# A block of three mixers in float32: long convolution in two parts, side work moved to the attention, softmax scale on a diagonal matrix

## The chip, the cores and the metric

The kernel runs on one core of one Trainium2 chip. The metric is the device time of one execution in microseconds (us); the median of several runs is compared. A profile is one execution of its own. The engines are named as in the profile: PE is TensorE's matmul, PEld its weight load, DVE is VectorE, ACT is ScalarE, POOL is GpSimd, SP the engine that issues nearly all loads.

## What is computed

One layer of a diffusion backbone for 256 latent tokens of width 2048, with 256 context tokens beside them. The normalised and modulated tokens go through one input projection, whose columns serve three mixers: neighbourhood attention (8 heads of 128, the local window and all context keys in one softmax), a two-dimensional Fourier transform, and a gated long convolution (Hyena, 512 channels, two convolutions one after the other). Each result is normalised, an output projection follows, and then a gated MLP. What the change touches, cut from the reference:

```python
q, k, v, f, hy = split_projection(h @ w_in[l])

def long_conv(z, k_spec, bias):
    y = jnp.fft.irfft(jnp.fft.rfft(zf, n=2 * L, axis=1) * k_spec, n=2 * L, axis=1)[:, :L]
    return (y + zf * bias).astype(z.dtype)

def hyena_mix(u, conv_w, conv_b, k_spec, bias):
    u = dwconv_centred(u, conv_w, conv_b)
    v, x1, x2 = jnp.split(u, HY_ORDER + 1, axis=-1)
    z = x1 * long_conv(v, k_spec[:, 0], bias[0])
    return x2 * long_conv(z, k_spec[:, 1], bias[1])

# in the attention, for each head
p = jax.nn.softmax(s, axis=-1)
out = p_local @ v_window + p_context @ v_context

# the modulation, of which the later parts are the kernel's side work
mod = silu(c) @ ada_w + ada_b
```

## The kernel before, in words

**Products with split weights.** The large products are done in three matmuls of a faster float32 form (mm3, line 164): weights and activations are each split into a high and a low part, and high x high, high x low and low x high are summed. A weight chunk is 4 x 128 rows by 512 columns. It arrives in two halves of 512 KB (Weights.loads, line 271) into eight raw buffers; ACT makes the high part w_hi (line 173) and DVE the low part w_lo (line 174) of each half; there are two split chunks (w1, line 307). Stream.get (line 294) sees to it that the next chunk's split is issued too. One chunk is 48 matmuls of 256 columns.

**Side work.** Three of the modulation's vectors are not needed at the start: G1, A2 and B2. ada_cols (line 342) computes them in 96 small steps, each a load of 512 KB (line 350) and one DVE instruction that multiplies it with the row s_row and sums it up (line 351). The steps wait in a list, and pump(n) (line 360) issues the next 2n of them. CFG says where: `p1` in the first stage, `win` as a fraction of a pump for each of the 24 chunks of the input projection (Stream.ready, line 298), `att` as pumps after each head, `wa` in the output projection's second half, and `rest` before the MLP. The side loads share the raw buffers and SP's queue with the weights.

**The projection and the long convolution** (lines 654 to 809). After keys and values come the Fourier columns, and then the steps named in `hyo`, in this order: u0, u1 and u2 are projections of four chunks each followed by the short convolution (project, line 789; conv, line 692), q0 and q1 the queries (line 796), l0 and l1 the two long convolutions, g0 and g1 the gates (line 786), n the group norm, m the bias's mask. longconv (line 752) turns z with transposes into zt, does the forward transform in fold (line 176: four float32 products of 512 columns, sums on DVE into X), multiplies with the filter's spectrum on DVE (lines 767 to 774, tiles X and Y), and does the inverse with 16 float32 products of 128 columns (line 780, tables gtab), which DVE adds to z (line 784).

**The attention** (lines 846 to 870). For each of 8 heads and each half t of the queries: one float32 product of 512 columns (line 850), bias and scale on DVE and ACT (lines 852, 853), the maximum on DVE (line 855), Exp with its sum on ACT (line 856), the reciprocal on DVE (line 857), the scaling of the 128 x 512 scores on DVE (line 858), four transposes of 128 x 128 on TensorE against the unit matrix `ident` (line 861), and a copy to PT on ACT (line 862). Then four products with the values (line 865). Between the heads, `pace` places chunks of the output projection's first half (wout_chunk, line 833), which reads the Fourier and Hyena results, yB.

**Order.** The program gives instructions in the order of the code; a list scheduler then fixes the order on each engine ahead of the run: of what its model of time holds for ready, it takes what stands earlier in the code. On the chip each engine runs its list in order.

Of the kernel before, what the change touches and what calls it, by code (L numbers as in the profile page):

```python
# [8 lines left out]
F32 = mybir.dt.float32  # L9
F32R = mybir.dt.float32r  # L10
AF = mybir.ActivationFunctionType
ALU = mybir.AluOpType
# [23 lines left out]
for _n, _k in V_LAYOUT:  # L36
# [9 lines left out]
    ns=2,  # L46
    p1=(0, 0, 2, 6, 9),
    blocks=(2, 2, 4, 4, 4),
    win=0.8,
    att=(1, 0, 1, 4, 0, 1, 0, 0),  # L50
    rest=99,
    start='hp pk x0 x1 h3 dc ft a00 a01 a10 a11 W wm si n1s wp n2s q0 ct c0 c1 f0 e s0 n0 e f1 e s1 e h0 w q1 n1 h1',
    warm=(8, 2),
# [1 line left out]
    g2=0.34,  # L55
    pace=(0, 2, 2, 2, 3, 4, 5, 5, 6),
    wo=1,
    hyo='b u0 l0 u1 g0 u2 l1 q0 g1 n q1 m',
    ia=1,
    ib=1,  # L60
    n0=-2.0,
# [64 lines left out]
def hybrid_block(ctx: ExitStack, tc: tile.TileContext, a: dict, out: bass.AP):  # L126
# [42 lines left out]
    def transpose(ps, src, n=P):  # L169
        nc.tensor.transpose(ps, src, ident[:n, :n])  # L170
# [576 lines left out]
    with ExitStack() as st:  # L747
        hp = pool(st, "hyena", 1, "right")
        u = [hp.tile([P, 4, L], F32, name=f"u{j}") for j in range(3)]
        z = u[0]  # L750

        def longconv(o):
            zt = hp.tile([P, 2, HYW], F32, tag="zt", name="zt")
            for t in range(2):
                ps = bank()
                for c in range(4):
                    transpose(ps[:, c * P : (c + 1) * P], z[:, c, t::2])
                nc.scalar.copy(zt[:, t, :], ps[:])
            X = hp.tile([P, 4, HYW], F32, tag="X", name="X")
            Y = hp.tile([P, 4, HYW], F32, tag="Y", name="Y")  # L760
            fold(zt, Y[:, 0:2, :], X)
            k = spec[:, o]
            def both(z):
                return z.unsqueeze(1).to_broadcast([P, 2, HYW])

            for h in range(2):
                TT(Y[:, h::2, :], both(X[:, h, :]), k[:, h::2, :], op=ALU.mult)  # L767
                TT(X[:, h, :], X[:, 2 + h, :], k[:, 2 + h, :], op=ALU.mult)
                TT(X[:, 2 + h, :], X[:, 2 + h, :], k[:, h, :], op=ALU.mult)
            TT(Y[:, 0:2, :], Y[:, 0:2, :], X[:, 0:2, :], op=ALU.subtract)  # L770
            TT(Y[:, 2:4, :], Y[:, 2:4, :], X[:, 2:4, :], op=ALU.add)
            for i, op in enumerate((ALU.add, ALU.subtract, ALU.subtract, ALU.add)):
                j = 2 * (i % 2)
                TT(X[:, i, :], Y[:, j, :], Y[:, j + 1, :], op=op)  # L774
            for c in range(0, 4, 2):
                ps = bank()
                for i in range(2):
                    for t in range(2):
                        for f in range(2):
                            mm(ps[:, i * L + t * P : i * L + (t + 1) * P], X[:, 2 * t + f, (c + i) * P : (c + i + 1) * P], gtab[:, 2 * t + f, :], f == 0, f == 1)  # L780
                for i in range(2):
                    b = vec[:, V_HYB + o * 4 + c + i : V_HYB + o * 4 + c + i + 1]
                    zc = z[:, c + i, :].rearrange("p (n t) -> p t n", t=2)
                    STT(zc, zc, b, ps[:, i * L : (i + 1) * L].rearrange("p (t n) -> p t n", t=2), op0=ALU.mult, op1=ALU.add)

        def gated(gate):
            TT(z[:], z[:], gate[:], op=ALU.mult)

        def project(j):
            pss = wide(stream, 4 + 4 * j, hx_hi, hx_lo)  # L790
            for i in range(4):
                n = 4 * j + i
                wv = [vec[:, V_HCW + 12 * q + n : V_HCW + 12 * q + n + 1] for q in range(3)]
                conv(pss[i // 2][:, (i % 2) * L : (i % 2 + 1) * L], u[j][:, i, :], *wv, vec[:, V_HCB + n : V_HCB + n + 1])

        def queries(j):
            pss = wide(stream, 16 + 4 * j, hx_hi, hx_lo)
            for h in range(2):
                nc.scalar.copy(flip(qT[:, 4 * j + 2 * h : 4 * j + 2 * h + 2, :].rearrange("p i n -> p (i n)")), pss[h].rearrange("p (r c) -> p r c", c=GW))

        steps = {
            "b": make_bias,
            "u0": lambda: project(0), "u1": lambda: project(1), "u2": lambda: project(2), "q0": lambda: queries(0), "q1": lambda: queries(1),
            "l0": lambda: longconv(0), "l1": lambda: longconv(1), "g0": lambda: gated(u[1]), "g1": lambda: gated(u[2]),
            "n": lambda: group_norm(hp, [z[:, i, :] for i in range(4)], V_MIX + 12, yB, None, 4, squares4(hp, z[:], "zt")),
            "m": mask_bias,
        }
        for step in CFG["hyo"].split():
            steps[step]()
# [10 lines left out]
    with ExitStack() as st:  # L820
        ap_ = pool(st, "att", 1, "right")
        yA_hi, yA_lo = (ap_.tile([P, 8, L], F32R, name=f"yA_{z}") for z in ("hi", "lo"))
        aT = ap_.tile([P, NH, L], F32, name="aT")
        yB_hi = ap_.tile([P, 8, L], F32R, name="yB_hi")
        yB_lo = ap_.tile([P, 8, L], F32R, name="yB_lo")
        for i in range(0, 8, 2):
            split(yB_hi[:, i : i + 2, :], yB_lo[:, i : i + 2, :], yB[:, i : i + 2, :])
        sqa = ap_.tile([P, L], F32, name="sqA")
        pad(ap_, PADS["att"])
        held = {}  # L830
        x_parts = []

        def wout_chunk(h, n, kc):
            yh, yl = ((yB_hi, yB_lo), (yA_hi, yA_lo))[h]
            if kc == 0:
                held[n] = [bank(acc_ps) for _ in range(2)]
            wide_chunk(stream, h * 8 + n * 2 + kc, held[n], yh, yl, kc * 4, kc == 0, kc == 1, h * kc == 1 and n == 3)
            if kc == 1:
                add_scaled(held[n], n, G1)
            if h == 1:  # L840
                pump(CFG["wa"][2 * n + kc])
            if h == 1 and kc == 1:
                square_parts(ap_, n, x_parts, "PT", 2)

        scale = 128.0 ** -0.5
        for hd in range(NH):
            PT = ap_.tile([P, 4, L], F32, tag="PT", name="PT", bufs=2)
            for t in range(2):
                ps = bank(acc_ps)
                mm(ps[:], qT[:, hd, t * P : (t + 1) * P], kT[:, hd, :], True, True)  # L850
                s = ap_.tile([P, 512], F32, tag="s", name="s", bufs=3)
                STT(s[:, :L], ps[:, :L], scale, bias[:, hd, 2 - 2 * t : 6 - 2 * t, :].rearrange("p m c -> p (m c)"), op0=ALU.mult, op1=ALU.add)
                nc.scalar.activation(s[:, L:], ps[:, L:], AF.Copy, scale=scale)
                sm = ap_.tile([P, 3], F32, tag="sm", name="sm", bufs=3)
                nc.vector.tensor_reduce(sm[:, 0:1], s[:], axis=AX.X, op=ALU.max, negate=True)
                nc.scalar.activation(s[:], s[:], AF.Exp, bias=sm[:, 0:1], accum_out=sm[:, 1:2])
                nc.vector.reciprocal(sm[:, 2:3], sm[:, 1:2])
                TS(s[:], s[:], sm[:, 2:3], None, op0=ALU.mult)
                ps = bank()
                for j in range(4):  # L860
                    transpose(ps[:, j * P : (j + 1) * P], s[:, j * P : (j + 1) * P])
                nc.scalar.copy(PT[:, :, t * P : (t + 1) * P], ps.rearrange("p (j n) -> p j n", n=P))
            ps = bank()
            for j in range(4):
                mm(ps[:, :L], v_t[:, j, hd * P : (hd + 1) * P], PT[:, j, :], j == 0, j == 3)
            nc.scalar.copy(flip(aT[:, hd, :]), ps[:, :L].rearrange("p (r c) -> p r c", c=GW))
            square_into(ap_, sqa, aT[:, hd, :], hd == 0)
            for c in range(CFG["pace"][hd], CFG["pace"][hd + 1]):
                wout_chunk(0, c // 2, c % 2)
            pump(CFG["att"][hd])  # L870
        group_norm(ap_, [aT[:, i, :] for i in range(NH)], V_MIX, yA_hi, yA_lo, 0, [sqa])
        for c in range(CFG["pace"][NH], 8):
            wout_chunk(0, c // 2, c % 2)
        for n in range(4):
            for kc in range(2):
                wout_chunk(1, n, kc)
        pump(CFG["rest"])
        rb2 = rms_bcast(ap_, x_parts, D, "r2", fill=(8, 5))
        STT(A2[:], A2[:], 1.0, vec[:, V_N2 : V_N2 + KT], op0=ALU.add, op1=ALU.mult)
        h2_hi = rtile("C", [P, KT, L], F32R, "h2_hi")  # L880
        h2_lo = rtile("D", [P, KT, L], F32R, "h2_lo")
        for k in range(KT):
            t = modulate(ap_, xr[:, k, :], A2[:, k : k + 1], rb2[:])
            shift_split(t, B2[:, k : k + 1], h2_hi[:, k, :], h2_lo[:, k, :])
# [178 lines left out]
```

## Time and profile before

| | us |
|---|---|
| median of three runs | 1299.75 (1296.78 to 1327.46) |
| the profiled execution's own time | 1298.77 |
| its span, first to last instruction | 1297.0 |
| TensorE busy in the span | 1271.9 (98%) |
| DVE busy | 887.0 (68%) |
| ACT busy | 557.6 (43%) |
| mean HBM traffic | 242 GB/s |

The keys and values take until about 281 us, the Fourier part and the projection with the long convolutions until about 431 us, the attention until about 505 us, the rest of the output projection until about 562 us, and the MLP to the end.

How to read the rows. In a list of groups stand line, engine, operation, output and inputs, size, count, then busy us and the mean ns of one, then the engine's idle time ahead of them and what ended it. In a table by stage stand the stretch and its length, then the busy us of PE, PEld, DVE, ACT and POOL with counts, the granted clock, the share of the DMA engines and GB/s. In an order of time stand the start, the duration, and the instruction, with the number of equal ones that were merged. In the chain that ended last stand start, duration and what was on it. In a list of waits stand who waited for whom, the total us, how many times, and the longest. A matmul's duration contains the way through the array, so that the durations of neighbours overlap; how many follow one another in a time is read from their starts.

### The profile page before, as it was taken

To read this page: it belongs to the slowest core of one execution; us is meant where nothing else is said; L and a number is where in the kernel's file an instruction comes from. 1 tells how busy PE (TensorE), PEld (TensorE's weight loads), DVE (VectorE), ACT (ScalarE), POOL (GpSimd) and SP (SyncE) were. 2 spreads that over 40 slices of the span, in tenths; PEclk is the share of its full clock that TensorE was granted. 3 is DMA by queue.
4 is the path that set the end of the run, shared out by engine and by line. 5 is a ranking of instruction groups with operands and counts; after the bars stand their busy time and mean duration, and the time that the engine had idled before them with its cause. 6 is when DMAs were issued, how large, how long until landed. Compare 5 with 4: busy or idle time off the path is not lost.

```text
span 1297.0 us, 24499 instructions
## 1 busy us (share of the span) xinstructions
PE 1271.9 (98%) x10290; PEld 1195.4 (92%) x10290; DVE 887.0 (68%) x1301; ACT 557.6 (43%) x736; POOL 0.9 (0%) x7
## 2 busy tenths in 40 slices
PE   9899999999989999999999999999999999999997
PEld 5677788899889889999999999999999999999997
DVE  5446678958999898987676767744446555655563
ACT  3532213134433665455444444433334444454443
POOL 0000000000000000000000000000000000000000
PEclk9999999999999999999999999999999999999999
DMA  9888787997678875756877777855556656665541
GB/s 349 340 323 290 297 339 291 338 281 286 219 256 309 326 240 181 259 173 220 273 251 267 252 263 254 297 194 194 192 194 193 192 193 193 194 194 195 194 163 65
DMA packets 94015, 315.28 MB, mean 243 GB/s; under 512 B 16080, under 2 KB 16336, under 8 KB 93264
## 3 DMA queue, kind: packets, MB, share of 16 engines
q1 hardware_dynamic: 93328, 312.65, 69.6%
q8 instruction: 80, 1.31, 0.4%
q10 hardware_dynamic: 576, 1.07, 0.2%
q14 instruction: 31, 0.25, 0.1%
HBM read 311.58 MB, written 2.10 MB: 242 GB/s over the span
## 4 chain that ended last, share of the span: by engine, by line
PE 88%; DVE 6%; DMA 2%; SPq 1%; ACT 1%; issue 1%; DVEq 0%; ACTq 0%
PE acc_ps L162 82%; PE mi_ps L162 3%; PE mi_ps L495 2%; DVE w_lo L174 1%; SPq L648 1%; PE mi_ps L170 1%; DMA raw<-in_ada_col_t 1%; DVE raw L351 1%; DMA raw<-in_w_in_t 1%; SPq L268 0%; ACT w_hi L173 0%; DMA pack<-in_pack 0%; ACT kT L461 0%; DVE Y L767 0%; DVE X L774 0%
## 5 line engine op out<-in xcount | busy, mean ns | idle before, releaser
L173 ACT CAST w_hi<-raw 128x1024 fp32r<-128x1024 f32 x376 | 380.6, 1049 | 517.8 <-PE acc_ps L162 464.8
L174 DVE TENSOR_TENSOR w_lo<-raw,w_hi 128x1024 fp32r<-128x1024 f32 x376 | 447.8, 1220 | 214.4 <-ACT w_hi L173 211.7
L162 PE MATMUL acc_ps<-h_hi,w_hi 128*128 128x256 f32 x1408 | 388.5, 276 | 0.5 <-ACT h_hi L256 0.5
L162 PE MATMUL acc_ps<-h_lo,w_hi 128*128 128x256 f32 x1408 | 388.8, 276 | 0.0
L162 PE MATMUL acc_ps<-h_hi,w_lo 128*128 128x256 f32 x1408 | 388.7, 276 | 0.0
L162 PEld LDWEIGHTS acc_ps<-h_hi,w_hi 128*128 128x128 f32 x1408 | 264.1, 188 | 0.7 <-ACT h_hi L256 0.7
L162 PEld LDWEIGHTS acc_ps<-h_lo,w_hi 128*128 128x128 f32 x1408 | 264.3, 188 | 0.0
L162 PEld LDWEIGHTS acc_ps<-h_hi,w_lo 128*128 128x128 f32 x1408 | 264.3, 188 | 0.0
L162 PE MATMUL acc_ps<-yh,w_lo 128*128 128x256 f32 x704 | 194.4, 276 | 0.0
L162 PE MATMUL acc_ps<-yl,w_hi 128*128 128x256 f32 x704 | 194.4, 276 | 0.0
L162 PE MATMUL acc_ps<-yh,w_hi 128*128 128x256 f32 x704 | 194.4, 276 | 0.0
L351 DVE SCALAR_TENSOR_TENSOR raw<-raw,s_row 128x1024 f32<-128x1024 f32 x128 | 154.2, 1217 | 35.7 <-DMA raw<-in_ada_col_t 35.5
L162 PE MATMUL acc_ps<-hx_hi,w_hi 128*128 128x256 f32 x512 | 142.9, 281 | 2.4 <-ACT hx_hi L256 2.4
L162 PE MATMUL acc_ps<-hx_hi,w_lo 128*128 128x256 f32 x512 | 141.9, 280 | 2.6 <-DVE w_lo L174 2.6
L162 PE MATMUL acc_ps<-hx_lo,w_hi 128*128 128x256 f32 x512 | 142.6, 280 | 0.0
L162 PEld LDWEIGHTS acc_ps<-yh,w_lo 128*128 128x128 f32 x704 | 132.2, 188 | 0.0
L162 PEld LDWEIGHTS acc_ps<-yh,w_hi 128*128 128x128 f32 x704 | 132.2, 188 | 0.0
L162 PEld LDWEIGHTS acc_ps<-yl,w_hi 128*128 128x128 f32 x704 | 132.2, 188 | 0.0
L162 PEld LDWEIGHTS acc_ps<-hx_hi,w_hi 128*128 128x128 f32 x512 | 96.1, 188 | 5.8 <-ACT hx_hi L256 2.9
L162 PEld LDWEIGHTS acc_ps<-hx_hi,w_lo 128*128 128x128 f32 x512 | 96.0, 189 | 5.3 <-DVE w_lo L174 3.4
L162 PEld LDWEIGHTS acc_ps<-hx_lo,w_hi 128*128 128x128 f32 x512 | 96.2, 188 | 1.5 <-DVE ht L252 0.8
L693 ACT ACTIVATE ga<-acc_ps,pack 128x256 f32<-128x256 f32 x44 | 23.8, 558 | 37.5 <-PE acc_ps L162 31.6
(237 smaller groups left out, 1528.3 us busy)
## 6 DMA issues: line engine op xcount, KB each, us to landing
raw<-in_ffn_t SPq DMA_DIRECT2D x264, 512.0 KB, 4.4
raw<-in_ada_col_t SPq DMA_DIRECT2D x128, 512.0 KB, 5.0
raw<-in_ada_t SPq DMA_DIRECT2D x64, 512.0 KB, 6.1
raw<-in_w_in_t SPq DMA_DIRECT2D x48, 512.0 KB, 5.5
raw<-in_w_kv_t SPq DMA_DIRECT2D x32, 512.0 KB, 5.6
raw<-in_w_out_t SPq DMA_DIRECT2D x32, 512.0 KB, 4.7
x_in<-in_xT SPq DMA_DIRECT2D x8, 256.0 KB, 5.4
kT<-in_c_tok SPq DMA_DIRECT2D x1, 2048.0 KB, 10.9
```

Source lines behind the costliest of these rows:

```text
L162: return nc.tensor.matmul(ps, lhsT, rhs, start=start, stop=stop, skip_group_check=True)
L170: nc.tensor.transpose(ps, src, ident[:n, :n])
L173: nc.scalar.copy(hi, src)
L174: TT(lo, src, hi.bitcast(F32), op=ALU.subtract)
L351: STT(r, r, 1.0, s_row[:, h * NA : (h + 1) * NA], op0=ALU.mult, op1=ALU.mult, accum_out=sums_[:, f, h : h + 1])
L495: return nc.tensor.matmul(ps[32 * j : 32 * j + 32, :w], s_t[:, kt, :], raws[i // nh][:, kt % nh, :], start=fresh, stop=q == last_q and i i ...
L648: nc.sync.dma_start(half[:, hd], src)
L693: nc.scalar.activation(dst, ps, AF.Identity, bias=b, scale=w1_)
```

## The change

Three things. The side work's shares: `win` from 0.8 to 0.6, `att` from a sum of 7 pumps to one of 12. The long convolution is cut into `forward` (transposes, transform, the work on the spectrum) and `inverse` (the 16 products and the sum onto z); the inverse stands one projection later in `hyo`: i0 behind u1 stays just ahead of the gate g0, and i1 comes behind q0. And in the attention the scores are no longer scaled: the unit matrix is, by ACT, with one factor per query, and the turning product is an ordinary matmul of the scores with this diagonal matrix.

```diff
-    win=0.8,
-    att=(1, 0, 1, 4, 0, 1, 0, 0),
+    win=0.6,
+    att=(1, 1, 2, 4, 1, 1, 1, 1),
...
-    hyo='b u0 l0 u1 g0 u2 l1 q0 g1 n q1 m',
+    hyo='b u0 l0 u1 i0 g0 u2 l1 q0 i1 g1 n q1 m',
...
-        def longconv(o):
+        held_X = {}
+
+        def forward(o):
             zt = hp.tile([P, 2, HYW], F32, tag="zt", name="zt")
...
                 TT(X[:, i, :], Y[:, j, :], Y[:, j + 1, :], op=op)
+            held_X[o] = X
+
+        def inverse(o):
+            X = held_X[o]
             for c in range(0, 4, 2):
                 ps = bank()
...
-            "l0": lambda: longconv(0), "l1": lambda: longconv(1),
+            "l0": lambda: forward(0), "l1": lambda: forward(1), "i0": lambda: inverse(0), "i1": lambda: inverse(1),
...
                 nc.vector.reciprocal(sm[:, 2:3], sm[:, 1:2])
-                TS(s[:], s[:], sm[:, 2:3], None, op0=ALU.mult)
+                inv = ap_.tile([P, P], F32, tag="inv", name="inv", bufs=2)
+                nc.scalar.activation(inv[:], ident, AF.Copy, scale=sm[:, 2:3])
                 ps = bank()
                 for j in range(4):
-                    transpose(ps[:, j * P : (j + 1) * P], s[:, j * P : (j + 1) * P])
+                    mm(ps[:, j * P : (j + 1) * P], s[:, j * P : (j + 1) * P], inv[:], True, True)
                 nc.scalar.copy(PT[:, :, t * P : (t + 1) * P], ps.rearrange("p (j n) -> p j n", n=P))
```

More of the change, by code (lines that the diff above doesn't have):

```diff
@@ L803, in hybrid_block @@
             "u0": lambda: project(0), "u1": lambda: project(1), "u2": lambda: project(2), "q0": lambda: queries(0), "q1": lambda: queries(1),
-            "l0": lambda: longconv(0), "l1": lambda: longconv(1), "g0": lambda: gated(u[1]), "g1": lambda: gated(u[2]),
+            "l0": lambda: forward(0), "l1": lambda: forward(1), "i0": lambda: inverse(0), "i1": lambda: inverse(1), "g0": lambda: gated(u[1]), "g1": lambda: gated(u[2]),
             "n": lambda: group_norm(hp, [z[:, i, :] for i in range(4)], V_MIX + 12, yB, None, 4, squares4(hp, z[:], "zt")),
```

## The prediction

> **What bounds the kernel now.** I read the engine totals first, then the chain that ended last, then the two stages that the change touches, each as a list of groups, and last the order of time around the places where TensorE stands.
>
> ```profile
> PE 1271.9 (98%) x10290; PEld 1195.4 (92%) x10290; DVE 887.0 (68%) x1301; ACT 557.6 (43%) x736; POOL 0.9 (0%) x7
> PE 88%; DVE 6%; DMA 2%; SPq 1%; ACT 1%; issue 1%; DVEq 0%; ACTq 0%
> 300.00:425.00 125.00, 119.87 (x969) 114.57 (x970) 121.67 (x190) 47.31 (x59) 0.00 (x0) 0.99 0.77 276
> 432.00:505.00 73.00, 72.85 (x483) 62.66 (x482) 65.64 (x133) 49.56 (x100) 0.00 (x0) 1.00 0.75 256
> ```
>
> The kernel is TensorE's from end to end. The third row is the projection with the long convolutions (300 to 425 us), the fourth the attention (432 to 505 us); after the length come the busy times of PE, PEld, DVE, ACT and POOL. DVE is full in the projection (121.67 of 125) and nearly so in the attention (65.64 of 73). But busy PE is not yet PE at work: durations overlap. So I take the spacing of matmuls from runs without a stall, and count.
>
> ```profile
> 564.76 718.55 PE acc_ps L162 x6336
> 284.89 7.07 PE L162 MATMUL mi_ps<-fl,AB 128*128 128x256 f32 x32
> 447.64 4.46 PE L162 MATMUL acc_ps<-kT,qT 128*128 128x512 f32 x10
> 440.90 0.60 PE L170 MATMUL mi_ps<-pack,s 128*128 128x128 f32 x4
> 342.53 2.43 PE L162 MATMUL mi_ps<-gtab,X 128*128 128x128 f32 x20
> 387.92 5.68 PE L162 MATMUL mi_ps<-gtab,X 128*128 128x128 f32 x32 [2.83 <-DVE X L774]
> L162 PE MATMUL acc_ps<-hx_lo,w_hi 128*128 128x256 f32 x285 | 79.5, 280 | 0.0
> L162 PE MATMUL acc_ps<-hx_hi,w_hi 128*128 128x256 f32 x285 | 79.4, 280 | 0.0
> L162 PE MATMUL acc_ps<-hx_hi,w_lo 128*128 128x256 f32 x287 | 79.2, 280 | 2.6 <-DVE w_lo L174 2.6
> L162 PE MATMUL mi_ps<-gtab,X 128*128 128x128 f32 x64 | 10.0, 318 | 2.9 <-DVE X L774 2.8
> L162 PE MATMUL mi_ps<-zt,ftab 128*128 128x512 f32 x16 | 7.2, 593 | 0.0
> L170 PE MATMUL mi_ps<-pack,u 128*128 128x128 f32 x16 | 2.6, 285 | 0.0
> L162 PE MATMUL mi_ps<-dg,ones 128*128 128x128 f32 x8 | 1.4, 294 | 0.1
> L162 PE MATMUL mi_ps<-ones,sqf 128*128 128x1 f32 x8 | 1.1, 253 | 0.2 <-DVE sqf L709 0.2
> ```
>
> First row: a matmul of the split weights takes 718.55 / 6336 = 0.1134 us. In the next rows the time is that of the run; taking off the last one's duration (0.28 us for 128 columns, 0.38 for 256, 0.59 for 512) and dividing by the rest gives 0.216 us for 256 float32 columns, 0.43 for 512, (0.60 - 0.28) / 3 = 0.107 for a transpose, (2.43 - 0.28) / 19 = 0.113 for a record of the inverse's 128-column products, and 0.174 in the second convolution, where they come as the DVE finishes X.
>
> Projection: 857 x 0.1134 + 64 x 0.113 + 16 x 0.43 + 16 x 0.107 + 16 x 0.113 = 114.9 us of work in 125. TensorE loses 10.1 us here, and that is all that this stage can give. Attention, by the same count:
>
> ```profile
> L162 PE MATMUL acc_ps<-yB_hi,w_hi 128*128 128x256 f32 x107 | 32.7, 308 | 0.0
> L162 PE MATMUL acc_ps<-yB_lo,w_hi 128*128 128x256 f32 x107 | 30.6, 287 | 0.0
> L162 PE MATMUL acc_ps<-yB_hi,w_lo 128*128 128x256 f32 x107 | 29.9, 280 | 0.0
> L162 PE MATMUL mi_ps<-PT,v_t 128*128 128x256 f32 x64 | 15.8, 390 | 0.1
> L162 PE MATMUL acc_ps<-kT,qT 128*128 128x512 f32 x30 | 14.2, 592 | 0.0
> L170 PE MATMUL mi_ps<-pack,s 128*128 128x128 f32 x64 | 9.3, 275 | 0.0
> L858 DVE TENSOR_SCALAR s<-s,sm 128x512 f32<-128x512 f32 x16 | 7.5, 480 | 0.1
> L351 DVE SCALAR_TENSOR_TENSOR raw<-raw,s_row 128x1024 f32<-128x1024 f32 x16 | 19.3, 1215 | 1.1 <-DMA raw<-in_ada_col_t 1.1
> L351 DVE DVE_READ_ACCUMULATOR raw<-raw,s_row 128x1 f32 x15 | 1.2, 82 | 0.0
> L717 ACT ACTIVATE sqt<-aT 128x256 f32<-128x256 f32 x7 | 2.9, 419 | 0.2
> L856 ACT ACTIVATE s<-s,sm 128x512 f32<-128x512 f32 x16 | 11.5, 722 | 7.4 <-DVE sm L855 7.4
> ```
>
> 321 x 0.1134 + 64 x 0.216 + 30 x 0.43 + 64 x 0.107 = 69.9 us in 73: TensorE is idle for 3 us at most. Whatever is added to it in the attention lengthens the kernel.
>
> **The softmax's scale on the diagonal.** The 16 TENSOR_SCALAR of 0.480 us leave DVE (7.5 us). In their place ACT makes 16 scaled unit matrices of 128 x 128, and the 64 transposes become 64 ordinary float32 products. The first is a gain for an engine that does not set the end, the last a cost for the one that does. How much? The code of the inverse calls 2 x 2 x 2 x 2 x 2 = 32 products of 128 float32 columns (convolutions, pairs of channel tiles, tiles, parities, frequency parts), and the trace holds 64 records of them; PT's 8 x 4 = 32 products are 64 records too. The 8 x 2 x 4 = 64 transposes are 64 records. So an ordinary product costs 2 x 0.113 = 0.226 us where the transpose costs 0.107: 64 x 0.119 = **+7.6 us**. Bounds: if a product with the diagonal went as one record, 64 x 0.006 = 0.4 us; if it ran like the stalled inverse at 387.92, 64 x (0.348 - 0.107) = 15.4 us. I take 7.6, since in the attention the operands lie ready and other matmuls fill the queue, as at 342.53.
>
> A rule speaks against this edit still more. The Trainium skill's page "TensorE: Matmul & The Clock Gate" (Terms) says that the transpose mode is four times faster for float32; by that alone the edit would cost an estimated 64 x 3 x 0.107 = 20.5 us. The rows above give 0.226 against 0.107, a factor of two at 128 columns; I keep the rows for the sum, and the rule as a rival.
>
> ACT's new operation is not in the trace at this size: the 128 x 256 ACTIVATE of 0.419 us bounds it above and zero below; 0.3 us lies on the line between, so 4.8 us, at most 6.7, on an engine that is busy for 49.56 of 73 us. It waits for the reciprocal, as Exp now waits for the maximum (7.4 us in all); queued behind it on ACT are the casts w_hi and the copies of PT, and w_lo on DVE and then TensorE wait for these. If each of the 16 also waits out one side step on DVE, 16 x 1.3 = 20.8 us, ACT holds 49.6 + 6.7 + 20.8 = 77.1 us in a stage of 73 + 7.6 = 80.6: still covered, so I cost it at nothing. Without that cover each wait would come onto TensorE.
>
> **The moved side work.** `win` 0.8 to 0.6 over 24 chunks turns 19 calls of pump into 14; `att` goes from a sum of 7 to 12. A call is two steps, so ten steps move: ten loads of 512 KB on SP's queue, ten multiply-and-sum of 1.215 us and ten reads of the accumulator of 0.082 us, 13.0 us of DVE. In the projection DVE falls from 121.67 to about 109 us. In the attention it becomes 65.6 - 7.5 + 13.0 = 71.1 of 80.6 us, so it still does not set the stage, with 9.5 us to spare. The ten loads now stand on SP's queue among w_out's, and both take the same eight raw buffers; the traffic becomes (256 x 73 + 5240) / 80.6 = 297 GB/s, against 276 in the projection, which I take as free. The waits for side data so far:
>
> ```profile
> DVE raw L351 <- DMA raw<-in_ada_col_t: 35.5, 18, 3.7
> DVE raw L351 <- DMA raw<-in_ada_col_t: 1.1, 1, 1.1
> ```
>
> First the whole trace, then 425 to 505 us: one wait in that stage. So nothing is added there.
>
> **The inverse behind the next projection.** It adds no instruction. What can it win? Look at DVE around TensorE's longest wait:
>
> ```profile
> 372.34 1.22 DVE L351 SCALAR_TENSOR_TENSOR raw<-raw,s_row 128x1024 f32<-128x1024 f32 x1
> ...
> 373.49 0.48 DVE L694 SCALAR_TENSOR_TENSOR u<-acc_ps,pack,u 128x255 f32<-128x255 f32 x1
> ...
> 387.09 2.49 DVE L774 TENSOR_TENSOR X<-Y 128x512 f32<-128x512 f32 x4
> 389.50 1.22 DVE L174 TENSOR_TENSOR w_lo<-raw,w_hi 128x1024 fp32r<-128x1024 f32 x1
> ```
>
> From 373.49 to 389.50 DVE works off u2's convolution and the whole forward part; only then does it split the next half chunk of weights (389.50 to 390.72). TensorE, which has used up its split weights at 385.09, waits 2.83 us for X and then does the 32 records at 0.174. With the inverse behind q0 it would have q0's next weights to go on with, but these come later than X: the forward part stands ahead of them in the program as before. So the 2.83 us mostly stay, under the name w_lo; what is won is the slow spacing, 31 x (0.174 - 0.113) = 1.9 us. The lighter DVE wins more: the side step at 372.34 delays u2's convolution by about 1 us, and of the 2.6 us that matmuls of the projection wait for w_lo I take half, 1.3 us, as due to side steps ahead of them. Sum **-4.2 us**. Bounds: nothing, and all 10.1 us.
>
> **The sum.** The profiled execution took 1298.77 us, 1297.0 of it span; it lies 0.98 us below the median of the three runs, 1299.75. 1298.8 + 7.6 - 4.2 = **1302.2 us** (span 1300.4). With the bounds: 1298.8 + 0.4 - 10.1 = 1289.1 and 1298.8 + 15.4 = 1314.2.
>
> **The rivals.**
> - The projection gives all. With DVE relieved the wait for X and every other gap goes (10.1 us), and the attention's 3 us of idle time absorb part of the new matmuls: 1298.8 + 7.6 - 10.1 - 3 = 1293.3 us. For it: DVE is at 97% there and is what TensorE waits for. Against it: 4.3 of the 10.1 us stand under no wait in these rows.
> - The split wins nothing: the wait moves from X to w_lo in full, and the order of the matmuls comes out much as it was. 1298.8 + 7.6 = 1306.4 us. For it stands w_lo at 389.50.
> - The diagonal is as cheap as a transpose (one record): 1298.8 + 0.4 - 4.2 = 1295.0 us. Against it are the doubled records of every float32 product.
> - The dear product, by four times the transpose or by the spacing of 387.92: 1310 to 1298.8 + 20.5 - 4.2 = 1315.1 us, the latter being what the page's rule would give. Against it is the row at 342.53.
> - Slower: DVE held by side loads in the attention. DVE works in order; with 26 side steps in that stage and 9.5 us to spare, it decides once a step waits 0.37 us on average for its data. At the mean of the waits in the trace, 35.5 / 18 = 2.0 us, it would be 52 - 9.5 = 42 us on TensorE, by late w_lo: 1344 us. For it: raw buffers are shared and SP is in order. Against it: one wait of 1.1 us in 16 steps so far.
>
> **How the numbers follow.** Forecast 0.43, projection gives all 0.20, split wins nothing 0.22, cheap diagonal 0.06, dear product 0.06, held DVE 0.03. The forecast's own range is 1297 to 1308. To leave out no more than two in ten, and for the bounds of the new product, the range is 1291 to 1314. A change of 2%, 26 us, is about what a measurement of this kernel can tell from none; only the held DVE reaches it, and nothing above reaches 26 us of gain: faster 0.01, same 0.95, slower 0.04.
>
> **What would show it.** Right: 128 records of the product s with inv, 0.11 us apart, in place of 64; the stage from the first score to the last PT longer by about 7 us; the TENSOR_SCALAR gone and 16 ACTIVATE of about 0.3 us; a wait of TensorE for w_lo near the second forward part where X stood; DVE below 92% in the projection. Wrong: 64 records, or a spacing over 0.15; TensorE without gaps from 300 to 425 us; waits of raw for the side loads between 430 and 510 us of more than 5 us.

## The result and the profile after

The changed kernel is slower by 0.65%: ratio 1.0065, with a 95% interval of 1.0049 to 1.0080, which on 1300 us is 8.5 us (6.4 to 10.4). Five of its nine runs, and some of the kernel before, took about 26 us longer whatever the kernel; they are left out of every ratio here, and the other four took 1307.5 to 1308.8 us. The profiled execution took 1308.38 us.

First the totals of the changed kernel's page, then its two stages (length, busy PE, PEld, DVE, ACT, POOL). The attention's stretch is taken 7 us longer than the one shown of before, by what the forecast adds to the stage.

```profile
PE 1284.3 (98%) x10354; PEld 1207.7 (92%) x10354; DVE 883.4 (68%) x1285; ACT 563.5 (43%) x752; POOL 0.9 (0%) x7
```

```profile
300.00:425.00 125.00, 121.27 (x973) 116.26 (x973) 111.26 (x164) 47.98 (x60) 0.00 (x0) 0.99 0.71 242
432.00:512.00 80.00, 78.97 (x523) 67.84 (x522) 67.41 (x136) 52.60 (x114) 0.00 (x0) 1.00 0.78 274
```

TensorE has 64 records more (10354 against 10290). DVE in the projection is down from 121.67 to 111.26 us, and yet TensorE does little more there: 973 matmuls against 969. In the attention TensorE is nearly as full as before.

To place the time I take the start of three instructions that both traces hold: the first matmul of the Fourier part (row of the time order), the first score product (the tile qT; the row's two last times are first and last start), and the first matmul of the MLP (row of the chain). Before:

```profile
L162 PE MATMUL acc_ps<-kT,qT x32: 590/592/596, 430.8 to 488.8; 128*128 128x512 f32 x32
```

After, in the same three views:

```profile
286.03 7.07 PE L162 MATMUL mi_ps<-fl,AB 128*128 128x256 f32 x32
```

```profile
L162 PE MATMUL acc_ps<-kT,qT x32: 590/592/595, 430.6 to 496.5; 128*128 128x512 f32 x32
```

```profile
573.85 718.56 PE acc_ps L162 x6336
```

Up to the Fourier part the changed kernel's execution is 286.03 - 284.89 = 1.1 us behind, although four of the ten moved side steps are gone from this stretch (38 on DVE against 42). TensorE's granted clock was 0.98 on average there, against 0.99 before, which is about 3 us in 286; so this difference says little about the change. From there to the scores it takes 144.6 us against 145.9, so it wins 1.3. From the scores to the MLP it takes 573.85 - 430.6 = 143.3 us against 134.0, so it loses 9.3. The MLP's row is the same to 0.01 us. The cost sits in the attention and the output projection; the projection gives little. Of the 9.3 us the new records explain 7.6. Of the other 1.7, 0.9 is a wait for yB's low part that the kernel before does not have; the rest stays open.

```profile
434.46 0.38 PE L162 MATMUL acc_ps<-yB_lo,w_hi 128*128 128x256 f32 x1 [0.92 <-DVE yB_lo L174]
```

In the attention, the groups of the product with the diagonal matrix, of the matrix itself and of the side steps, from 425 to 520 us:

```profile
L351 DVE SCALAR_TENSOR_TENSOR raw<-raw,s_row 128x1024 f32<-128x1024 f32 x27 | 32.6, 1217 | 4.2 <-DMA raw<-in_ada_col_t 4.2
L162 PE MATMUL mi_ps<-inv,s 128*128 128x128 f32 x128 | 16.9, 280 | 0.1
L865 ACT ACTIVATE inv<-pack,sm 128x128 f32<-128x128 f32 x16 | 6.1, 401 | 2.3 <-DVE sm L863 2.3
```

One run of sixteen of these matmuls, and the second inverse with the wait ahead of it, in the order of time on TensorE; then DVE around that wait:

```profile
503.14 1.95 PE L162 MATMUL mi_ps<-inv,s 128*128 128x128 f32 x16
387.63 4.59 PE L162 MATMUL mi_ps<-gtab,X 128*128 128x128 f32 x24 [3.08 <-DVE X L776]
```

```profile
386.80 2.49 DVE L776 TENSOR_TENSOR X<-Y 128x512 f32<-128x512 f32 x4
389.20 3.49 DVE L174 TENSOR_TENSOR w_lo<-raw,w_hi 128x1024 fp32r<-128x1024 f32 x3
```

There are 128 records where 64 transposes stood, (1.95 - 0.28) / 15 = 0.111 us apart. The wait for X, 2.83 us before, is 3.08 us. The inverse may now stand behind q0, but q0's next low parts still begin only after X, at 389.20, so TensorE has nothing else and takes the inverse's first 24 records here all the same, at (4.59 - 0.28) / 23 = 0.187 us.

The prediction put the slow spacing of this inverse down to DVE, which was just finishing X. The granted clock says something else. It is the third number from the right in a table by stage; first three stretches of before (the first inverse, the second, and the projection's matmuls after it), then two of the changed kernel (the second inverse, and the matmuls after it):

```profile
342.50:344.50 2.00, 2.00 (x20) 2.00 (x19) 2.00 (x2) 0.00 (x0) 0.00 (x0) 1.00 0.03 8
390.00:392.00 2.00, 2.00 (x11) 2.00 (x11) 1.86 (x3) 0.00 (x0) 0.00 (x0) 0.50 0.17 25
394.00:396.00 2.00, 2.00 (x20) 2.00 (x19) 2.00 (x4) 0.14 (x1) 0.00 (x0) 1.00 0.57 223
```

```profile
388.50:390.50 2.00, 2.00 (x11) 2.00 (x11) 2.00 (x4) 0.00 (x0) 0.00 (x0) 0.50 0.00 0
392.00:394.00 2.00, 2.00 (x19) 2.00 (x19) 2.00 (x4) 0.00 (x0) 0.00 (x0) 1.00 0.85 330
```

Soon after TensorE has stood for X, its clock is at half for a while in both kernels, and in 2 us it does 11 matmuls in place of 19 or 20. X was complete at 389.58 in before (387.09 + 2.49), and the spacing stayed slow beyond 391. Whatever TensorE does in such a stretch is slow, the inverse or other matmuls, so moving the inverse away from there does not win the time back.

### The profile page after: what moved, and what is told of

It reads as the page before. It is cut to its first block, busy times and chain, and to the rows that moved or that the text cites. A ratio compares the mean times of both kernels' runs of the same rounds, so it can differ in the third digit from the quotient of the medians.

```text
span 1306.6 us, 24614 instructions
## 1 busy us (share of the span) xinstructions
PE 1284.3 (98%) x10354; PEld 1207.7 (92%) x10354; DVE 883.4 (68%) x1285; ACT 563.5 (43%) x752; POOL 0.9 (0%) x7
## 4 chain that ended last, share of the span: by engine, by line
PE 90%; DVE 5%; DMA 2%; ACT 1%; issue 1%; DVEq 0%; ACTq 0%; SPq 0%
PE acc_ps L162 82%; PE mi_ps L162 6%; PE mi_ps L495 2%; DMA raw<-in_ada_col_t 1%; DVE w_lo L174 1%; DVE raw L351 1%; PE mi_ps L170 0%; ACT w_hi L173 0%; DMA pack<-in_pack 0%; DVE part L248 0%; DMA raw<-in_w_out_t 0%; ACT kT L461 0%; DVE xr L673 0%; DVE Y L769 0%; DVE o_tok L976 0%
## 5 line engine op out<-in xcount | busy, mean ns | idle before, releaser
L162 PE MATMUL acc_ps<-hx_hi,w_hi 128*128 128x256 f32 x512 | 144.6, 284 | 3.0 <-ACT hx_hi L256 2.4
L162 PE MATMUL acc_ps<-hx_hi,w_lo 128*128 128x256 f32 x512 | 144.8, 284 | 0.0
```

Of the source, the lines that this page charges most:

```text
L162: return nc.tensor.matmul(ps, lhsT, rhs, start=start, stop=stop, skip_group_check=True)
```

## The experiments

All were measured beside the kernel before, on the same chip. My theory: the diagonal costs TensorE its 64 more records, about 7.6 us; the cut wins nothing, because the order of DVE's work keeps TensorE waiting; the moved side work wins a little. The rivals: the loss comes from the side work in the attention, or from ACT's wait for the reciprocal; the cut does win and something hides it.

### Each part alone

**The diagonal matrix alone**

```diff
-                TS(s[:], s[:], sm[:, 2:3], None, op0=ALU.mult)
+                inv = ap_.tile([P, P], F32, tag="inv", name="inv", bufs=2)
+                nc.scalar.activation(inv[:], ident, AF.Copy, scale=sm[:, 2:3])
...
-                    transpose(ps[:, j * P : (j + 1) * P], s[:, j * P : (j + 1) * P])
+                    mm(ps[:, j * P : (j + 1) * P], s[:, j * P : (j + 1) * P], inv[:], True, True)
```

> Only the diagonal matrix is changed against the kernel before. Theory (TensorE pays for 64 more matmul records at 0.113 us, less what a transpose took): 7.6 us slower than before, 6 to 10. Rival (the attention's 9.3 us come mainly from the ten more side steps on DVE and their loads): 4 us slower at most, since DVE is even relieved of 7.5 us here.

Measured: ratio 1.0068 (1.0056 to 1.0081), 8.8 us slower. That is as much as the whole change costs, with no side step moved, and with DVE relieved. In its chain, the MLP starts here:

```profile
575.69 718.55 PE acc_ps L162 x6336
```

Its first score product starts at 430.8 us, as before; the loss is all behind that. ACT's new step holds TensorE up little in this trace: it waits for inv once, for 0.5 us.

**The cut alone**

```diff
-    hyo='b u0 l0 u1 g0 u2 l1 q0 g1 n q1 m',
+    hyo='b u0 l0 u1 i0 g0 u2 l1 q0 i1 g1 n q1 m',
```

with forward and inverse as in the change.

> Only the long convolution is cut in two and the inverse placed one projection later. Theory (the wait for X stays, since the next half chunk's low part is made behind the forward part): within 1.5 us of before, with TensorE still waiting about 3 us after the second forward part. Rival (the cut removes the wait and what the side steps do hides it): 3 to 6 us faster.

Measured: ratio 1.0015 (1.0002 to 1.0029), 2.0 us slower. TensorE's waits from 300 to 425 us, and where the second of them comes from, in the order of time on DVE:

```profile
PE mi_ps L162 <- DVE X L776: 2.7, 1, 2.7
PE acc_ps L162 <- DVE w_lo L174: 2.7, 1, 2.7
```

```profile
349.26 0.86 DVE L694 SCALAR_TENSOR_TENSOR u<-acc_ps,pack,u 128x255 f32<-128x255 f32 x2
...
352.79 1.26 DVE L790 SCALAR_TENSOR_TENSOR u<-u,pack,mi_ps 128x256 f32<-128x256 f32 x3
353.96 1.22 DVE L174 TENSOR_TENSOR w_lo<-raw,w_hi 128x1024 fp32r<-128x1024 f32 x1
```

The wait for X is as it was, and there is a new one of 2.7 us, longer than all the short waits for w_lo that the kernel before had there (2.6 us in four, one of them ahead of 300 us): the first inverse's sums onto z (line 790 here) now fall together with u1's short convolution, and the two hold back the low part of TensorE's next weights until 353.96. The cut did not take the wait for X away, and it made one. Whether that is where the 2.0 us go is not shown: by the three starts used above, this trace takes 146.3 us from the Fourier part to the scores (before 145.9) and 136.6 from there to the MLP (before 134.0).

**The side work alone**

```diff
-    win=0.8,
-    att=(1, 0, 1, 4, 0, 1, 0, 0),
+    win=0.6,
+    att=(1, 1, 2, 4, 1, 1, 1, 1),
```

> Only ten side steps are moved from the projection to the attention. Theory: the projection gains 1 to 2 us, the attention loses at most 1.5 us, together within 1.5 us of before. Rival (side loads hold DVE in the attention): 2 us slower or more, with waits of DVE for side loads of over 5 us between 430 and 510 us.

Measured: ratio 0.9980 (0.9966 to 0.9993), 2.6 us faster, a little past what I expected. TensorE's waits from 300 to 425 us and the stages:

```profile
PE mi_ps L162 <- DVE X L774: 1.4, 1, 1.4
PE acc_ps L162 <- ACT w_hi L173: 0.6, 1, 0.6
```

```profile
300.00:425.00 125.00, 122.99 (x996) 115.80 (x994) 114.28 (x172) 52.01 (x67) 0.00 (x0) 1.00 0.74 255
425.00:505.00 80.00, 77.38 (x515) 67.47 (x515) 77.20 (x156) 49.56 (x99) 0.00 (x0) 0.98 0.82 283
```

All waits for w_lo are gone from this stretch, and the one for X is half as long; the granted clock stays at 1.00 here. But in the attention DVE is at 77.20 of 80 us, and this does cost something. The three starts, then the first product that needs yB's low part, DVE ahead of it, and two stretches of the table by stage behind it:

```profile
282.07 7.07 PE L162 MATMUL mi_ps<-fl,AB 128*128 128x256 f32 x32
L162 PE MATMUL acc_ps<-kT,qT x32: 590/592/595, 422.1 to 484.6; 128*128 128x512 f32 x32
561.07 0.73 PE L162 MATMUL acc_ps<-h_hi,w_hi 128*128 128x256 f32 x4
```

```profile
427.48 0.39 PE L162 MATMUL acc_ps<-yB_lo,w_hi 128*128 128x256 f32 x1 [2.39 <-DVE yB_lo L174]
```

```profile
425.59 1.23 DVE L351 SCALAR_TENSOR_TENSOR raw<-raw,s_row 128x1024 f32<-128x1024 f32 x1 [0.74 <-DMA raw<-in_ada_col_t]
426.74 2.49 DVE L174 TENSOR_TENSOR yB_lo<-yB,yB_hi 128x512 fp32r<-128x512 f32 x4
```

```profile
428.00:430.00 2.00, 2.00 (x11) 2.00 (x10) 2.00 (x6) 0.40 (x2) 0.00 (x0) 0.50 1.04 438
432.00:434.00 2.00, 2.00 (x20) 2.00 (x20) 2.00 (x4) 1.18 (x4) 0.00 (x0) 1.00 1.03 420
```

From the Fourier part to the scores it takes 140.0 us against 145.9, so it wins 5.9; from there to the MLP 139.0 against 134.0, so it loses 5.0. A side step that waited 0.74 us for its load stands on DVE ahead of the split of yB, TensorE waits 2.39 us for it, and behind that its clock is at half (and once more just ahead of the MLP, from 558 to 560 us). This wait, of 0.9 to 2.4 us, is in every trace with the moved side work and in none without it. Between scores and MLP the four traces with the moved side work and without the diagonal take 136.3 to 140.7 us, the kernel before, the cut alone and the earlier split of q0's weights alone (below) 134.0 to 136.6: that something is lost there is shown by the wait, its size only roughly.

So the three parts are +8.8, +2.0 and -2.6 us, together +8.2; the change measured +8.5.

**The change without the diagonal**

The cut and the side work, with line 858's scaling and the transposes as before; run twice.

> The changed kernel without its diagonal: scores scaled on DVE and transposed as before, the cut and the moved side work kept. Theory: 1.5 us faster than before (from 3 faster to 0.5 slower), that is about 9 us faster than the changed kernel. Rival (the side work in the attention costs what the diagonal does not): 2 us or more slower than before.

> The same kernel as split_side, whose runs gave no interval: the cut and the moved side work, without the diagonal. Theory (the parts add up: cut 2.0 us slower, side work 2.6 us faster): within 1.5 us of before. Rival (cut and side work disturb one another): 3 us slower or more.

The first gave no interval. The second: ratio 1.0004 (0.9982 to 1.0025), no difference from before, which fits the sum of the two parts (-0.6 us); the rival's 3 us lie at the very end of the interval. In its trace the wait for X is 2.4 us, followed by the clock at half, and the stretch from the Fourier part to the scores takes 144.0 us: with the cut, most of the 5.9 us that the side work alone wins there are gone. Why the wait stays long with the cut is not shown. Against the changed kernel's 1.0065 it shows once more that the loss hangs on the diagonal.

### What of the diagonal costs

**Ordinary products with the plain unit matrix**

```diff
-                    transpose(ps[:, j * P : (j + 1) * P], s[:, j * P : (j + 1) * P])
+                    mm(ps[:, j * P : (j + 1) * P], s[:, j * P : (j + 1) * P], ident, True, True)
```

The scaling on DVE stays, and ACT makes no matrix.

> The kernel before, its 64 transposes written as ordinary products with the plain unit matrix; DVE scales the scores as before, ACT makes no matrix. Theory (the diagonal's 8.9 us are TensorE's doubled records): 7.6 us slower than before, 6 to 10. Rival (a good part is ACT's wait for the reciprocal and its 16 new instructions): at most 5 us slower.

**Each product with the diagonal twice**

```diff
                 for j in range(4):
-                    mm(ps[:, j * P : (j + 1) * P], s[:, j * P : (j + 1) * P], inv[:], True, True)
+                    for _ in range(2):
+                        mm(ps[:, j * P : (j + 1) * P], s[:, j * P : (j + 1) * P], inv[:], True, True)
```

> The changed kernel with each of the 64 products with the diagonal matrix done twice (the second writes the same again). Theory (each record costs 0.113 us of a full TensorE): 128 records more, 14.5 us on top of the changed kernel's 8.5, together 23 us slower than before, 21 to 26. Rival (the cost lies in waits around the product, not in its records): 5 us on top at most, 14 us together.

Measured: with the plain unit matrix ratio 1.0088 (1.0023 to 1.0152), 11 us slower with a wide interval; its profiled span is 1306.2 us against 1297.0, 9.2 us longer. With the doubled product ratio 1.0200 (1.0180 to 1.0220), 26 us slower than before, so 17.5 us more than the changed kernel. The rows of the product in the first, and in the second (425 to 540 us) with the wait that is new there:

```profile
L162 PE MATMUL mi_ps<-pack,s 128*128 128x128 f32 x128 | 17.0, 278 | 0.0
```

```profile
L162 PE MATMUL mi_ps<-inv,s 128*128 128x128 f32 x256 | 30.7, 277 | 0.2 <-ACT inv L865 0.2
L162 PE MATMUL acc_ps<-yA_hi,w_hi 128*128 128x256 f32 x6 | 1.9, 342 | 2.3 <-ACT yA_hi L173 2.3
```

The same operands, scores and unit matrix, make 64 records as a transpose and 128 as an ordinary product: it is the kind of product that doubles them, not the scaled matrix. And 128 further records cost 128 x 0.113 = 14.5 us, with a new wait of 2.3 us for yA_hi 16.8, of the 17.5 measured. With that the cost is shown to lie in TensorE's records. How much of the 8.8 us beyond 7.6 is ACT's does not come out of these times, since the interval with the unit matrix is too wide; that TensorE waited for inv for only 0.5 us in the trace of the diagonal alone speaks for little.

**Scaling on ACT, transposes kept**

```diff
-                TS(s[:], s[:], sm[:, 2:3], None, op0=ALU.mult)
+                nc.scalar.activation(s[:], s[:], AF.Copy, scale=sm[:, 2:3])
```

on top of the moved side work alone.

> The moved side work alone, without the cut, and the scores scaled by ACT instead of DVE, with the transposes kept. Theory (TensorE sets the attention's length, DVE's 7.5 us are hidden): like the moved side work alone, 2.6 us faster than before, 1 to 4. Rival (in the attention DVE holds TensorE up once the side work is there): 5 us faster or more.

Measured: ratio 0.9991 (0.9960 to 1.0022). There is no sign of a further gain from taking 7.5 us off DVE; the interval just reaches the rival's 5 us, so it speaks against the rival without closing it.

### What holds TensorE in the projection

**The next weights split ahead of the second forward part**

```diff
-    hyo='b u0 l0 u1 i0 g0 u2 l1 q0 i1 g1 n q1 m',
+    hyo='b u0 l0 u1 i0 g0 u2 r l1 q0 i1 g1 n q1 m',
...
+            "r": lambda: stream.ready(17, 1),
```

Chunk 17 is q0's second. This was run with cut and side work, with the side work alone, and alone on the kernel before.

> The changed kernel without its diagonal, and with the split of q0's second weight chunk placed ahead of the second forward part in the program. Theory (TensorE waits there because these weights come behind the forward part on DVE): its wait after the second forward part falls from 2.8 us to under 1 us, and the whole is 1 to 4 us faster than before. Rival (DVE is the bound there, and X later by two splits moves the wait elsewhere): no faster than before, with the same 3 us of waits under another name.

> The moved side work, without cut and without diagonal, and q0's second weight chunk split ahead of the second long convolution. Theory (the two gains are of one stage but of different waits: side steps ahead of w_lo, and the forward part ahead of w_lo): 3 to 6 us faster than before, with a wait of TensorE behind the second forward part of under 1.2 us. Rival (both gains are the same slack of DVE): no better than the moved side work alone, 1 to 3 us faster.

> The kernel before with nothing but q0's second weight chunk split ahead of the second long convolution. Theory (the 2.8 us of waiting are due to the order of DVE's work, not to where the inverse stands): the wait falls to about 1 us and the whole is 1 to 3 us faster than before. Rival (DVE full, so that two splits earlier make X later by as much): within 0.7 us of before, with the wait as long as it was.

Measured: ratios 0.9980 (0.9957 to 1.0003), 0.9984 (0.9967 to 1.0001) and 0.9995 (0.9977 to 1.0013); no interval excludes that nothing changed. With cut and side work it is 3.1 us better than without the earlier split (1.0004), but the two intervals overlap. TensorE's waits from 300 to 425 us, first with the side work, then alone:

```profile
PE acc_ps L162 <- ACT w_hi L173: 0.6, 1, 0.6
PE mi_ps L162 <- DVE X L774: 0.3, 1, 0.3
```

```profile
PE mi_ps L162 <- DVE X L774: 2.3, 1, 2.3
PE acc_ps L162 <- DVE w_lo L174: 1.3, 3, 0.6
```

With the side work the wait is gone, as expected (0.3 us), but the time is that of the moved side work alone (2.1 us faster than before, against 2.6): the rival was right there. Alone the order shortens the wait by only 0.5 us, and the time by nothing measurable; in that trace the clock stays at 1.00 behind the wait of 2.3 us, so such a wait is not always followed by the slower clock, and these traces do not tell what decides it. So my reading was half right: TensorE waits because DVE comes late with either X or w_lo, and the order decides which of the two is late; but how late depends on how much DVE has to do. That the wait merely moves elsewhere is not shown: from the Fourier part to the scores this trace takes 140.8 us, the side work alone 140.0.

**Twice as many side steps moved**

```diff
-    win=0.8,
-    att=(1, 0, 1, 4, 0, 1, 0, 0),
+    win=0.4,
+    att=(2, 2, 3, 4, 1, 2, 2, 1),
```

> Scores scaled and turned as before, no cut, and twice as many side steps moved: win 0.4, and 17 pumps in the attention in place of 7. Theory (with ten steps moved DVE is busy for 77.2 of 80 us of the attention, so ten more steps, 13 us, are over its limit and come late to TensorE, while the projection has 3 us left to give): 4 to 12 us slower than before. Rival (DVE's work only slides into the next stage): within 2 us of before.

Measured: ratio 1.0097 (1.0078 to 1.0115), 12.6 us slower. The attention's stretch, the waits from 420 to 530 us, and SP's issues in the order of time:

```profile
425.00:505.00 80.00, 71.85 (x449) 59.77 (x448) 75.83 (x150) 45.56 (x93) 0.00 (x0) 0.96 0.85 303
```

```profile
ACT s L853 <- DVE s L852: 7.2, 4, 3.1
...
ACT w_hi L173 <- DMA raw<-in_w_out_t: 6.8, 6, 1.7
...
PE acc_ps L162 <- ACT s L853: 3.9, 2, 2.9
...
DVE raw L351 <- DMA raw<-in_ada_col_t: 1.4, 1, 1.4
```

```profile
424.75 15.14 SPq L268 DMA_DIRECT2D raw<-in_ada_col_t  x8
...
446.28 14.44 SPq L268 DMA_DIRECT2D raw<-in_ada_col_t  x8
...
469.62 17.88 SPq L268 DMA_DIRECT2D raw<-in_ada_col_t  x8
488.40 2.27 SPq L268 DMA_DIRECT2D raw<-in_w_out_t  x2
```

Then DVE ahead of one of TensorE's longest waits, that wait, and a stretch of the table by stage behind it:

```profile
468.36 1.22 DVE L351 SCALAR_TENSOR_TENSOR raw<-raw,s_row 128x1024 f32<-128x1024 f32 x1
...
471.27 0.75 DVE L852 SCALAR_TENSOR_TENSOR s<-acc_ps,bias 128x256 f32<-128x256 f32 x2
```

```profile
472.16 2.07 PE L162 MATMUL acc_ps<-kT,qT 128*128 128x512 f32 x2 [2.93 <-ACT s L853]
```

```profile
476.00:478.00 2.00, 2.00 (x12) 2.00 (x11) 2.00 (x6) 1.55 (x5) 0.00 (x0) 0.50 0.68 277
```

TensorE does 449 matmuls in 80 us instead of 515. The size is a little above what was expected. DVE is no busier than with ten steps (75.83 against 77.20 us) and hardly waits for side data, but its order is what TensorE waits for: from 462.25 to 471.35 us seven side steps run on DVE, and only then line 852 of the next scores; ACT waits for that (7.2 us in all), and TensorE for ACT to free the scores' bank (3.9 us). So the side steps do hold TensorE up, as the theory had it. Beside this, ACT waits for the output projection's own weights, six times: SP now issues three rows of eight side loads, where the kernel before has one (14.47 us, from 438.57), and the weights' loads stand behind them. And such waits are followed by the slower clock: it averages 0.96 from 425 to 505 us and 0.93 from 505 to 580 us, and 1.00 in the kernel before. That is at most 8 us of the 22 us that this trace loses between scores and MLP (156.1 us against 134.0).

## Why the prediction was right, and where it was off

The forecast was 3.4 us slower within a range of 1291 to 1314; measured were 8.5 us slower and 1308 us. The direction and the cost of the diagonal were right. The stated range held the result, but the forecast's own range, 1297 to 1308, only reaches it at its end: of the 5.1 us between forecast and result, 3.6 are the projection's term and 1.2 the diagonal's. Point by point:

- **What bounds the kernel.** Right: TensorE is full in the attention, and what was added to it there came out in the time.
- **The diagonal, +7.6 us.** Right in kind: doubled records at 0.111 us. Alone it measured 8.8 us (7.3 to 10.5). The page's factor of four (the Trainium skill, "TensorE: Matmul & The Clock Gate", Terms) is not what these runs show: at 128 columns the ordinary product costs 2 x 0.111 us against 0.107 for the transpose, a factor of two, and the 20.5 us estimated from the page lie outside the interval.
- **ACT's new matrix.** 0.401 us, near the upper bound and not the 0.3 that I took; its wait for the reciprocal was 2.3 us in all, against the 20.8 that I allowed for. ACT stayed at 52.6 of 80 us.
- **The side work.** The ten steps did move, four of them from ahead of the Fourier part. That nothing is added in the attention was wrong: DVE's waits for side data grew to 4.2 us in three, a side step stands ahead of yB's low part, and TensorE waits for that, 0.9 us here and 2.4 with the side work alone. The rival of the held DVE was right in kind and far too dear at this dose; at twice the dose it cost 12.6 us, by DVE's side steps ahead of the scores, by late weights and by the slower clock.
- **The projection, -4.2 us: this term failed.** The prediction had it that the wait of 2.83 us stays and that the slow spacing of the inverse, 1.9 us, is won. The wait did stay, and kept the name X where w_lo was expected. The spacing did not get better (0.187 against 0.174): it was misread as DVE finishing X, and is the granted clock of 0.50 behind the wait, which stays with it. The upper bound of the diagonal, 15.4 us, was taken from that same spacing, so it rests on a stretch at half clock. The cut alone costs 2.0 us (0.3 to 3.8). The side work's part, 2.3 us in the prediction (1.0 and 1.3), measured 2.6 in the whole; that the two agree is luck, since its trace wins 5.9 us in the projection and loses 5.0 behind it. Together the projection's two edits are worth -0.6 us, not -4.2.

The rival "the split wins nothing" (1306.4 us) came nearest to the result: it puts the cut and the side work together at nothing, and they measured -0.6 us.

The version that beats both kernels is the moved side work alone: 0.9980 (0.9966 to 0.9993) of the kernel before, and about 11 us faster than the changed one.

## What to carry to other kernels

Where TensorE is full, work moved onto it from any other engine costs its full time, however much that engine is relieved: count the records that the trace holds per call before replacing a transpose by an ordinary float32 product. A wait named after one tile can be that of another one that stands behind it on the same engine; ask what the waiting engine would do instead, and whether that is ready. Background work costs a stage as soon as one of its steps, or its loads, stands ahead of what that stage waits for, so look at the order on the engine and on the queue, not only at how busy they are. And when matmuls come slowly, read the granted clock of that very stretch before blaming the engine that feeds them: a wait can cost more than its own length.

## What the runs showed of the hardware

- A float32 matmul of 128 columns is two records of 0.111 us here, with the plain unit matrix as with the scaled one; with the same operands a transpose is one, at 0.107 us (128 against 64 records with the plain unit matrix).
- An ACTIVATE on 128 x 128 with a factor per partition took 0.401 us; one on twice the columns, a Square without such a factor, took 0.419 us (128 x 256).
- Behind waits of TensorE of 2.3 to 3.1 us its granted clock was seen at 0.50: with the side work alone, the matmuls from 427.70 to 431.08 us start 0.211 us apart, against 0.113 at a clock of 1.00. A stretch of 3.4 us at half the clock costs about 1.7 us. Behind another wait of 2.3 us, in the run of the earlier split alone, it stayed at 1.00.
